# A recurrence kernel's small triangular solves on GpSimd alone, with permuted head slots and two masked evictions

## Chip, cores and metric

One core of a Trainium2 chip runs the whole program. The metric is the device time of one execution in microseconds, lower is better. Engines: TensorE (PE), VectorE (DVE), ScalarE (ACT), GpSimd (POOL), SyncE (SP, which here only issues DMAs).

## What is computed

A two-layer backbone on 2048 tokens of width 1024, with a prefix of 256 context tokens. The first layer is a bidirectional RWKV-7 recurrence with 16 heads of 64, the second a multi-head latent attention. The part that matters here is the recurrence, run over the context tokens and then over the others, forward and backward in time:

```python
def step(s, inp):                       # s: (direction, batch, head, 64, 64)
    r_t, lw_t, k_t, v_t, a_t, b_t = inp
    sa = jnp.einsum('dbhij,dbhj->dbhi', s, a_t)
    s = s * jnp.exp(lw_t)[..., None, :] + sa[..., None] * b_t[..., None, :] + v_t[..., None] * k_t[..., None, :]
    return s, jnp.einsum('dbhij,dbhj->dbhi', s, r_t)
```

In front of it stand the projections of r, k, v and the decays, behind it a normalisation, a gate and an output projection.

## The kernel before

The work goes through stages that overlap a little. **Projection** (project_block): a context block of 256 tokens, then four blocks of 512. In a block, PE multiplies in units of 128 channels, first the k units, then r and v. Each product is made of three matmuls with split operands: activations lh + ll, weights whi + wlo. ScalarE casts whi and lh, GpSimd or DVE subtracts to get wlo (L418) and ll (L493). The k units also give, per direction, the chunk matrices that the scan needs (GpSimd: kd L627, kb L630, the copy EC L620).

**Scan** (scan): the recurrence in chunks. One iteration advances each direction by 32 tokens: x (L1122, from the state S), u (L1132, multiplies x by a triangular inverse), the next state s (L1150), y (L1160). The state tile svu holds for each head the old state, the loaded v and the copied u, and s contracts over all of it. Ahead of each chunk aa (L1092) makes 16 products of 64x64, which are evicted times a mask into the tile big (L1097), and tr (L1106) makes transposes, which ScalarE evicts (L1110). EC is the decay by which s is evicted (L1153). PE's order is written by hand: per iteration the steps of one direction stand between those of the other, with matmuls of another task as filler. The filler is the gate's projection in iterations 0 to 47 (weights f_whi by ScalarE, f_wlo L695 on DVE and L696 on GpSimd, three buffers each), then the readout (L790 and after). The other engines are ordered by a scheduler from priorities; keep_in_program_order pins an instruction against it.

**Solve**: four chunks of 32 tokens in two directions and 16 heads make 128 systems of 32x32, one per partition. solve(n) loads their matrix Lt (L987), sets N to the identity and in 31 steps adds to N's later columns a product of one column of N with one row of Lt: a multiply (L1002) and an add (L1006) per step. Rows 0 to 5 of N (Na, tmpa) are on DVE, rows 6 to 31 (Nb, tmpb) on GpSimd, and the multiplies of even steps are pinned to the program's order. solve is a generator: its caller takes two steps at a time between other work, solves 0 and 1 during the projection (L546, L576), solve n+2 during the four iterations after the start of n. N goes to memory and comes back transposed as tt (load_tt). There are 18 solves, and the scan waits for none of them but through tt.

The u copies (L1138 on DVE, L1140 on ScalarE) write heads in steps of two slots:

```python
dst = S[ur, e, cls // 2:8:2, :]
```

so the DVE copy of a half and the ScalarE copy of the same half interleave in one region of the tile.

Of the kernel before, what the change touches and what calls it, by code (L numbers as in the profile page):

```python
# [43 lines left out]
PIN = 0  # L44
# [64 lines left out]
def revlast(ap):  # L109
    step, n = ap.ap[-1]  # L110
    return bass.AP(ap.tensor, ap.offset + step * (n - 1), [list(x) for x in ap.ap[:-1]] + [[-step, n]])

# [9 lines left out]
class Build:  # L122
# [348 lines left out]
    def project_block(self, t0, W, bp, wp, tp, pp, ind, indt, smask, w2d, sol):  # L471
# [85 lines left out]
        def v_unit(f, lh, ll):  # L557
# [15 lines left out]
            for e in range(2):  # L573
                nc.sync.dma_start(self.vtok[t0:t0 + W, e, f, :].rearrange("(n p) d -> p n d", p=P), vk[:, :W // P, e * 64:(e + 1) * 64])
# [8 lines left out]
        for f in range(KT):  # L583
# [13 lines left out]
            for d in range(2):  # L597
# [22 lines left out]
                nc.gpsimd.tensor_copy(self.EC[d][:, f, c0:c0 + nch], E[:, :nch, 32 - one])  # L620
# [362 lines left out]
    def solve(self, n):  # L983
        nc, sp, Nd = self.nc, self.svp, self.Nd
        JS = 6
        L = sp.tile([P, 32, 32], F32, name="Lt")
        nc.sync.dma_start(L.rearrange("p s t -> p (s t)"), self.Ld[n])  # L987
        Na = sp.tile([P, JS, 32], F32, name="Na")
        Nb = sp.tile([P, 32 - JS, 32], F32, name="Nb")
        nc.gpsimd.memset(Na, 0.0)  # L990
        nc.gpsimd.memset(bass.AP(Na.tensor, Na.offset, [Na.ap[0], [33, JS]]), 1.0)
        nc.gpsimd.memset(Nb, 0.0)
        nc.gpsimd.memset(bass.AP(Nb.tensor, Nb.offset + JS, [Nb.ap[0], [33, 32 - JS]]), 1.0)
        for s in range(31):
            for eng, N, j0, j1 in ((nc.vector, Na, 0, min(s + 1, JS)), (nc.gpsimd, Nb, JS, s + 1)):
                k = j1 - j0
                if k <= 0:
                    continue
                w = 31 - s
                tmp = sp.tile([P, 160 if j0 == 0 else 176], F32, name="tmpa" if j0 == 0 else "tmpb")  # L1000
                tv = tmp[:, :k * w].rearrange("p (j t) -> p j t", t=w)
                op = eng.tensor_tensor(tv, N[:, 0:k, s:s + 1].to_broadcast([P, k, w]),  # L1002
                                       L[:, s, s + 1:32].unsqueeze(1).to_broadcast([P, k, w]), ALU.mult)
                if s % 2 == PIN:
                    self.tc.keep_in_program_order(op)
                eng.tensor_tensor(N[:, 0:k, s + 1:32], N[:, 0:k, s + 1:32], tv, ALU.add)  # L1006
            if s % 2:
                yield
        yield
        nc.sync.dma_start(Nd[n % 2][0:JS].rearrange("j p t -> p j t"), Na)  # L1010
        nc.sync.dma_start(Nd[n % 2][JS:32].rearrange("j p t -> p j t"), Nb)
# [9 lines left out]
    def scan(self, upto):  # L1021
        nc, ins, tc = self.nc, self.ins, self.tc
        JS = 6
        HP_CHAIN, HP_AA = 3000, 1500
        with ExitStack() as top:
# [55 lines left out]
            def aa(d, i):  # L1081
# [5 lines left out]
                with tc.high_priority(HP_AA):  # L1087
                    ps = [pp.tile([P, 4, 64], F32, name="ps_aa", bufs=3) for _ in range(2)]
                    for p in range(8):
                        for e in range(2):  # L1090
                            o, r = slice(64 * ((e + p + 1) % 2), 64 * ((e + p + 1) % 2) + 64), slice(64 * e, 64 * e + 64)
                            nc.tensor.matmul(ps[e][o, p // 2, :], kb[r, p, ck], B[r, 2 * p + e, 0, ck], start=True, stop=True)  # L1092
                    for e in range(2):
                        r = slice(64, 128) if e == 0 else slice(0, 64)
                        for p0 in range(2):
                            o = slice(64 * ((e + p0 + 1) % 2), 64 * ((e + p0 + 1) % 2) + 64)
                            nc.vector.tensor_tensor(B[r, 2 * p0 + e::4, 0, ck], ps[e][o], amask[o, d:d + 1, :].to_broadcast([64, 4, 64]), ALU.mult)  # L1097
# [19 lines left out]
            def x_of(d, i):  # L1117
                (B, k), S = big(d, i), SVU[d][i % 2]
                xp = pp.tile([P, 4, 64], F32, name="ps_xu", bufs=2)
                for h in range(NH):  # L1120
                    r = slice(32 * (h % 4), 32 * (h % 4) + 32)
                    nc.tensor.matmul(xp[r, h // 4, :], B[:, h, 0, k:k + 32], S[:, h % 2, h // 2, :], start=True, stop=True)  # L1122
# [793 lines left out]
```

## Time and profile before

| what | value |
|---|---|
| runs | 5520.90, 5520.99, 5532.20 us; median 5520.99 |
| profiled execution | 5527.81 us, span 5526.0 us, mean granted clock 0.922 |
| PE / PE weight load | 4724.3 us (85%) / 3434.1 us (62%) |
| DVE / ACT / POOL | 3784.7 us (68%) / 2186.3 us (40%) / 2752.4 us (50%) |
| projection, scan, then latent attention | to about 1326, 1331 to about 2750, to 5526 us |

Busy times are those of the whole span, and the stages differ: what a change in one stage is worth is read from that stage. A row of the waits says how long an engine stood still and which instruction released it. Idle time of an engine for which nobody waits costs nothing.

### The profile page before, as it was taken

The page shows a single profiled execution, that of the slowest core. Times are in us where ns is not written, and L with a number is a line of the kernel's source. Part 1 is how long each engine was busy: PE and PEld are TensorE (multiplying, and loading weights), DVE is VectorE, ACT ScalarE, POOL GpSimd, SP SyncE. Part 2 cuts the span into 40 slices and gives each one's busy share as a digit, 9 for nine tenths or more (in the row PEclk, how much of TensorE's full clock was granted, in tenths as well). Part 3 has the DMA queues.
Part 4 walks back from the last instruction along what each step waited for, and adds up shares of the span by engine and source line. Part 5 has one row for each costly group of instructions (what it writes and reads, how often), then busy time and mean ns, then how long its engine had stood idle before and what let it go on. Part 6 is the DMA issues. An engine that isn't in the chain of part 4 may idle for free.

```text
span 5526.0 us, 123424 instructions
## 1 busy us (share of the span) xinstructions
PE 4724.3 (85%) x50559; PEld 3434.1 (62%) x50559; DVE 3784.7 (68%) x6213; ACT 2186.3 (40%) x3862; POOL 2752.4 (50%) x2473
## 2 busy tenths in 40 slices
PE   6778787887878887677789998699999999999999
PEld 4655555555767776466667876555555555555567
DVE  5989897875888888786565443266666666666644
ACT  4444444443544444333333343233333333333332
POOL 2575656463544444343254452255656655656551
PEclk8889898887989999788889999889999999999999
DMA  7655555556776666868788767621111111011023
GB/s 220 188 168 171 162 165 172 165 169 188 212 214 175 186 178 168 243 196 235 229 247 256 246 163 237 235 76 54 30 50 58 28 51 57 23 58 32 25 91 104
DMA packets 1006881, 818.59 MB, mean 148 GB/s; under 512 B 280885, under 2 KB 876420, under 8 KB 994794
## 3 DMA queue, kind: packets, MB, share of 16 engines
q1 hardware_dynamic: 872046, 734.48, 44.5%
q10 hardware_dynamic: 134188, 75.95, 5.0%
q8 instruction: 397, 6.50, 0.5%
q14 instruction: 170, 1.39, 0.1%
q0 software_dynamic: 80, 0.26, 0.0%
HBM read 551.84 MB, written 258.66 MB: 147 GB/s over the span
## 4 chain that ended last, share of the span: by engine, by line
PE 31%; DVE 9%; DMA 3%; ACT 2%; issue 2%; POOL 2%; SPq 1%; ACTq 0%; DVEq 0%; POOLq 0%
PE ps_o L1729 9%; PE ps_s L1706 7%; PE ps_p L1680 4%; DVE mx L1684 3%; DVE ri L1745 2%; DVE acc L1722 1%; PE ps_a L1387 1%; PE ps_a L1388 1%; PE ps_a L1389 1%; ACT pt L1708 1%; PE ps_o L1882 1%; PE ps_o L1884 1%; PE ps_o L1883 1%; DVE acc L1719 1%; PE ps_p L1694 1%
## 5 line engine op out<-in xcount | busy, mean ns | idle before, releaser
L1722 POOL TENSOR_TENSOR acc<-acc,pt 128x1024 f32<-128x1024 f32 x352 | 867.2, 2464 | 406.5 <-ACT pt L1708 386.5
L1684 DVE TENSOR_REDUCE mx<-ps_p 128x1 f32<-128x512 f32 x1024 | 661.5, 682 | 356.8 <-PE ps_p L1680 356.7
L1708 ACT ACTIVATE pt<-ps_s 128x1024 f32<-128x1024 f32 x576 | 591.0, 1026 | 779.8 <-PE ps_s L1706 737.6
L1706 PE MATMUL ps_s<-qr,a_kr 64*128 64x512 f32 (+1 forms) x2304 | 524.6, 393 | 5.8 <-ACT qr L1697 4.0
L1729 PE MATMUL ps_o<-pt,av 128*64 128x512 f32 x2304 | 523.3, 599 | 0.0
L1680 PE MATMUL ps_p<-knh,qnh 64*128 64x512 f32 (+1 forms) x1280 | 369.9, 404 | 99.3 <-DVE mx L1684 48.9
L500 PE MATMUL ps_r<-lh,whi 128*128 128x512 f32 (+1 forms) x960 | 386.4, 404 | 37.0 <-ACT lh L492 33.4
L418 POOL TENSOR_TENSOR wlo<-wraw,whi 128x1024 fp32r<-128x1024 f32 (+3 forms) x120 | 265.7, 2215 | 300.2 <-ACT whi L414 293.8
L501 PE MATMUL ps_r<-ll,whi 128*128 128x512 f32 (+1 forms) x960 | 382.7, 400 | 15.4 <-DVE ll L493 11.9
L502 PE MATMUL ps_r<-lh,wlo 128*128 128x512 f32 (+1 forms) x960 | 379.6, 397 | 12.9 <-POOL wlo L418 7.1
L696 POOL TENSOR_TENSOR f_wlo<-f_wraw,f_whi 128x384 fp32r<-128x384 f32 x118 | 158.8, 1347 | 384.4 <-ACT f_whi L694 320.0
L1729 PEld LDWEIGHTS ps_o<-pt,av 128*64 128x64 f32 x2304 | 154.3, 137 | 296.3 <-issue 292.2
L1680 PE MATMUL ps_p<-a_kr,qr 64*128 64x512 f32 (+1 forms) x1280 | 329.5, 391 | 1.5 <-DMA qr<-qr 1.5
L1706 PEld LDWEIGHTS ps_s<-qr,a_kr 64*128 64x128 f32 (+1 forms) x2304 | 289.9, 185 | 64.3 <-DVE qr L1697 15.2
L1680 PEld LDWEIGHTS ps_p<-knh,qnh 64*128 64x128 f32 x1280 | 184.3, 189 | 196.8 <-DVE mx L1684 132.2
L480 DVE SCALAR_TENSOR_TENSOR lerp<-xx,cols,hb 128x512 f32<-128x512 f32 (+1 forms) x240 | 239.3, 1022 | 88.2 <-POOL ll L493 67.9
L1706 PE MATMUL ps_s<-qnh,knl 64*128 64x512 f32 x1152 | 283.0, 417 | 4.3 <-ACT pt L1708 4.2
L1150 PE MATMUL ps_s<-svu,big 128*64 128x64 f32 x4544 | 236.7, 247 | 52.0 <-DVE svu L1138 30.3
L1706 PE MATMUL ps_s<-qnh,knh 64*128 64x512 f32 x1152 | 267.5, 389 | 0.0
L1706 PE MATMUL ps_s<-qnl,knh 64*128 64x512 f32 x1152 | 267.4, 389 | 0.0
L1097 DVE TENSOR_TENSOR big<-ps_aa,amask 64x256 f32<-64x256 f32 x576 | 243.2, 422 | 29.7 <-PE ps_aa L1092 16.3
L1110 ACT COPY big<-ps_aa 64x256 f32<-64x256 f32 x576 | 211.0, 366 | 132.2 <-PE ps_aa L1106 126.2
(342 smaller groups left out, 12550.1 us busy)
## 6 DMA issues: line engine op xcount, KB each, us to landing
f_w<-wod SPq DMA_DIRECT2D x72, 1024.0 KB
wraw<-rwkv_w_in SPq DMA_DIRECT2D x120, 512.0 KB
kbt<-KB SPq DMA_DIRECT2D x72, 512.0 KB
big<-AR SPq DMA_DIRECT2D x144, 256.0 KB
AR<-ar SPq DMA_DIRECT2D x64, 512.0 KB
KB<-kb SPq DMA_DIRECT2D x64, 512.0 KB
f_wraw<-rwkv_w_in SPq DMA_DIRECT2D x64, 512.0 KB
f_wraw<-mla_w_in SPq DMA_DIRECT2D x54, 512.0 KB
```

The costliest lines, as they stand in the source:

```text
L418: eng.tensor_tensor(lo[:, k0:k1, :], raw[:, k0:k1, :], hi[:, k0:k1, :].bitcast(F32), ALU.subtract)
L480: nc.vector.scalar_tensor_tensor(L[:, :W], xx[:, k, :W], col["mu"][:, j * 8 + k:j * 8 + k + 1], hb[:, k, 1:W + 1], ALU.mult, ALU.add)
L500: nc.tensor.matmul(ps, hi[:, k, :], lh[k][:, :W], start=k == 0, stop=False)
L501: nc.tensor.matmul(ps, hi[:, k, :], ll[k][:, :W], start=False, stop=False)
L502: nc.tensor.matmul(ps, lo[:, k, :], lh[k][:, :W], start=False, stop=k == KT - 1)
L1097: nc.vector.tensor_tensor(B[r, 2 * p0 + e::4, 0, ck], ps[e][o], amask[o, d:d + 1, :].to_broadcast([64, 4, 64]), ALU.mult)
L1680: nc.tensor.matmul(ps[h2][:, o * kw:(o + 1) * kw], x[r, t * P:(t + 1) * P], y[r, k0:k0 + kw], start=st, stop=not st)
L1684: nc.vector.tensor_reduce(mx[:, h2, t, n % 4:n % 4 + 1], ps[h2], mybir.AxisListType.X, ALU.max)
L1706: nc.tensor.matmul(ps[:, h2, :], x[r, ks], y[r, :], start=i == 0, stop=i == 4)
L1708: nc.scalar.activation(pt, ps, AF.Exp, scale=SCALE)
L1722: eng.tensor_tensor(a, a, pt, ALU.add)
L1729: nc.tensor.matmul(st["po"][hs, :], st["v"][:, kt, hs], pt[:, h2, :], start=kt == 0, stop=kt == NK - 1)
```

## The change

The solve no longer splits N's rows. One tile Nt (32x32 per partition) and one temporary tmpn of 256 elements, all 62 operations on GpSimd, two memsets instead of four, one store instead of two; no instruction is pinned. The heads of svu, EC and the token copy of v take a permuted slot, 4(f mod 2) + f div 2, so a u copy writes four slots in a row: DVE's and ScalarE's halves are separate. aa writes the eight products of one operand half into one PSUM tile of 64 partitions (two of the four 64x64 quarters of the array instead of four), and each of two evictions takes a 64x512 region instead of four that take 64x256.

```diff
--- before.py
+++ after.py
@@ -41,7 +41,6 @@
 BREAK = 1000
 GB = 288
 FW, FS, FF = 2, 1, 1
-PIN = 0
 MU = 2
 
 _SHAPES = {
@@ -109,6 +108,10 @@
 def revlast(ap):
     step, n = ap.ap[-1]
     return bass.AP(ap.tensor, ap.offset + step * (n - 1), [list(x) for x in ap.ap[:-1]] + [[-step, n]])
+
+
+def slot(f):
+    return 4 * (f % 2) + f // 2
 
 
 def chunked(ap):
@@ -571,7 +574,7 @@
             vk = tp.tile([P, 4, P], F32, name="vk", tag="ta", bufs=2)
             nc.vector.tensor_copy(vk.rearrange("p n m -> p (n m)")[:, :W], pt[:, :W])
             for e in range(2):
-                nc.sync.dma_start(self.vtok[t0:t0 + W, e, f, :].rearrange("(n p) d -> p n d", p=P), vk[:, :W // P, e * 64:(e + 1) * 64])
+                nc.sync.dma_start(self.vtok[t0:t0 + W, e, slot(f), :].rearrange("(n p) d -> p n d", p=P), vk[:, :W // P, e * 64:(e + 1) * 64])
             next(sh[0], None)
             next(sol, None)
 
@@ -617,7 +620,7 @@
                 nc.scalar.activation(E[:, :nch, inc:inc + 32], chunked(cs[:, :W]), AF.Exp, scale=-KAPPA / 2)
                 Ei = tp.tile([P, 512], F32, name="Ei", bufs=2)
                 nc.scalar.activation(Ei[:, :W], cs[:, :W], AF.Exp, scale=KAPPA / 2)
-                nc.gpsimd.tensor_copy(self.EC[d][:, f, c0:c0 + nch], E[:, :nch, 32 - one])
+                nc.gpsimd.tensor_copy(self.EC[d][:, slot(f), c0:c0 + nch], E[:, :nch, 32 - one])
                 ar = tp.tile([P, 16, 64], F32, name="ar", bufs=2)
                 nc.vector.scalar_tensor_tensor(rc(ar[:, :nch, 0:32]), chunked(kkh[:, :W]), -2.0, E[:, :nch, exc:exc + 32], ALU.mult, ALU.mult)
                 nc.vector.tensor_tensor(ar[:, :nch, 32:64], chunked(psr[:, :W]), E[:, :nch, inc:inc + 32], ALU.mult)
@@ -981,34 +984,23 @@
         self.TT = {}
 
     def solve(self, n):
-        nc, sp, Nd = self.nc, self.svp, self.Nd
-        JS = 6
+        nc, sp, eng = self.nc, self.svp, self.nc.gpsimd
         L = sp.tile([P, 32, 32], F32, name="Lt")
         nc.sync.dma_start(L.rearrange("p s t -> p (s t)"), self.Ld[n])
-        Na = sp.tile([P, JS, 32], F32, name="Na")
-        Nb = sp.tile([P, 32 - JS, 32], F32, name="Nb")
-        nc.gpsimd.memset(Na, 0.0)
-        nc.gpsimd.memset(bass.AP(Na.tensor, Na.offset, [Na.ap[0], [33, JS]]), 1.0)
-        nc.gpsimd.memset(Nb, 0.0)
-        nc.gpsimd.memset(bass.AP(Nb.tensor, Nb.offset + JS, [Nb.ap[0], [33, 32 - JS]]), 1.0)
+        N = sp.tile([P, 32, 32], F32, name="Nt")
+        eng.memset(N, 0.0)
+        eng.memset(bass.AP(N.tensor, N.offset, [N.ap[0], [33, 32]]), 1.0)
         for s in range(31):
-            for eng, N, j0, j1 in ((nc.vector, Na, 0, min(s + 1, JS)), (nc.gpsimd, Nb, JS, s + 1)):
-                k = j1 - j0
-                if k <= 0:
-                    continue
-                w = 31 - s
-                tmp = sp.tile([P, 160 if j0 == 0 else 176], F32, name="tmpa" if j0 == 0 else "tmpb")
-                tv = tmp[:, :k * w].rearrange("p (j t) -> p j t", t=w)
-                op = eng.tensor_tensor(tv, N[:, 0:k, s:s + 1].to_broadcast([P, k, w]),
-                                       L[:, s, s + 1:32].unsqueeze(1).to_broadcast([P, k, w]), ALU.mult)
-                if s % 2 == PIN:
-                    self.tc.keep_in_program_order(op)
-                eng.tensor_tensor(N[:, 0:k, s + 1:32], N[:, 0:k, s + 1:32], tv, ALU.add)
+            k, w = s + 1, 31 - s
+            tmp = sp.tile([P, 256], F32, name="tmpn")
+            tv = tmp[:, :k * w].rearrange("p (j t) -> p j t", t=w)
+            eng.tensor_tensor(tv, N[:, 0:k, s:s + 1].to_broadcast([P, k, w]),
+                              L[:, s, s + 1:32].unsqueeze(1).to_broadcast([P, k, w]), ALU.mult)
+            eng.tensor_tensor(N[:, 0:k, s + 1:32], N[:, 0:k, s + 1:32], tv, ALU.add)
             if s % 2:
                 yield
         yield
-        nc.sync.dma_start(Nd[n % 2][0:JS].rearrange("j p t -> p j t"), Na)
-        nc.sync.dma_start(Nd[n % 2][JS:32].rearrange("j p t -> p j t"), Nb)
+        nc.sync.dma_start(self.Nd[n % 2].rearrange("j p t -> p j t"), N)
 
     def load_tt(self, n):
         nc = self.nc
@@ -1020,7 +1012,6 @@
 
     def scan(self, upto):
         nc, ins, tc = self.nc, self.ins, self.tc
-        JS = 6
         HP_CHAIN, HP_AA = 3000, 1500
         with ExitStack() as top:
             top.enter_context(tc.manual_schedule(engines={mybir.EngineType.PE}))
@@ -1085,16 +1076,14 @@
                 ck = slice(k0, k0 + 64)
                 kb = KBh[(d, i // 2)]
                 with tc.high_priority(HP_AA):
-                    ps = [pp.tile([P, 4, 64], F32, name="ps_aa", bufs=3) for _ in range(2)]
+                    ps = [pp.tile([P, 8, 64], F32, name="ps_aa", bufs=3) for _ in range(2)]
                     for p in range(8):
                         for e in range(2):
-                            o, r = slice(64 * ((e + p + 1) % 2), 64 * ((e + p + 1) % 2) + 64), slice(64 * e, 64 * e + 64)
-                            nc.tensor.matmul(ps[e][o, p // 2, :], kb[r, p, ck], B[r, 2 * p + e, 0, ck], start=True, stop=True)
+                            o, r = slice(64 - 64 * e, 128 - 64 * e), slice(64 * e, 64 * e + 64)
+                            nc.tensor.matmul(ps[e][o, p, :], kb[r, p, ck], B[r, 2 * p + e, 0, ck], start=True, stop=True)
                     for e in range(2):
-                        r = slice(64, 128) if e == 0 else slice(0, 64)
-                        for p0 in range(2):
-                            o = slice(64 * ((e + p0 + 1) % 2), 64 * ((e + p0 + 1) % 2) + 64)
-                            nc.vector.tensor_tensor(B[r, 2 * p0 + e::4, 0, ck], ps[e][o], amask[o, d:d + 1, :].to_broadcast([64, 4, 64]), ALU.mult)
+                        o = slice(64 - 64 * e, 128 - 64 * e)
+                        nc.vector.tensor_tensor(B[o, e::2, 0, ck], ps[e][o], amask[o, d:d + 1, :].to_broadcast([64, 8, 64]), ALU.mult)
 
             def tr(d, m, half):
                 if m >= NCH // 2:
@@ -1119,7 +1108,7 @@
                 xp = pp.tile([P, 4, 64], F32, name="ps_xu", bufs=2)
                 for h in range(NH):
                     r = slice(32 * (h % 4), 32 * (h % 4) + 32)
-                    nc.tensor.matmul(xp[r, h // 4, :], B[:, h, 0, k:k + 32], S[:, h % 2, h // 2, :], start=True, stop=True)
+                    nc.tensor.matmul(xp[r, h // 4, :], B[:, h, 0, k:k + 32], S[:, h % 2, slot(h // 2), :], start=True, stop=True)
                 X[d] = sp.tile([P, 4, 64], F32, name="xs")
                 nc.scalar.copy(X[d], xp)
 
@@ -1133,7 +1122,7 @@
                 for cls in range(4):
                     e = cls % 2
                     ur = slice(96, 128) if e == 0 else slice(32, 64)
-                    dst = S[ur, e, cls // 2:8:2, :]
+                    dst = S[ur, e, cls // 2 * 4:cls // 2 * 4 + 4, :]
                     if cls < 2:
                         nc.vector.tensor_copy(dst, up[32 * cls:32 * cls + 32, :, :])
                     else:
@@ -1147,7 +1136,7 @@
                 ps = pp.tile([P, 8, 64], F32, name="ps_s", bufs=1)
                 for h in range(NH):
                     e = h % 2
-                    nc.tensor.matmul(ps[e * 64:(e + 1) * 64, h // 2, :], B[:, h, 1, k:k + 64], S[:, e, h // 2, :], start=True, stop=True)
+                    nc.tensor.matmul(ps[e * 64:(e + 1) * 64, slot(h // 2), :], B[:, h, 1, k:k + 64], S[:, e, slot(h // 2), :], start=True, stop=True)
                 for e in range(2):
                     r = slice(e * 64, (e + 1) * 64)
                     nc.vector.tensor_tensor(nx[r, e, :, :], ps[r, :, :], self.EC[d][r, :, c:c + 1].to_broadcast([64, 8, 64]), ALU.mult)
@@ -1157,7 +1146,7 @@
                 yp = pp.tile([P, 4, 64], F32, name="ps_xu", bufs=2)
                 for h in range(NH):
                     cls, q = h % 4, h // 4
-                    nc.tensor.matmul(yp[32 * cls:32 * cls + 32, q, :], B[:, h, 0, k + 32:k + 64], S[:, h % 2, h // 2, :], start=True, stop=True)
+                    nc.tensor.matmul(yp[32 * cls:32 * cls + 32, q, :], B[:, h, 0, k + 32:k + 64], S[:, h % 2, slot(h // 2), :], start=True, stop=True)
                 ys = sp.tile([P, 4, 64], F32, name="ys")
                 nc.scalar.copy(ys, yp)
                 ylate.append(lambda: nc.scalar.dma_start(self.yd[c // 4][c % 4, d].rearrange("k t x -> (k t) x"), ys.rearrange("p q d -> p (q d)")))
```

On GpSimd, in the first full block of the projection, where the k units end; wlo is a weight split, tmpb and Nb are the solve's two operations, ll the split of an activation. Before:

```order
L418 TENSOR_TENSOR wlo<-wraw,whi 128x1024
L1002 TENSOR_TENSOR tmpb<-Nb,Lt 128x133
L1006 TENSOR_TENSOR Nb<-Nb,tmpb 128x7x19
L1002 TENSOR_TENSOR tmpb<-Nb,Lt 128x144
L1006 TENSOR_TENSOR Nb<-Nb,tmpb 128x8x18
L418 TENSOR_TENSOR wlo<-wraw,whi 128x1024
L1002 TENSOR_TENSOR tmpb<-Nb,Lt 128x153
L1006 TENSOR_TENSOR Nb<-Nb,tmpb 128x9x17
L1002 TENSOR_TENSOR tmpb<-Nb,Lt 128x160
L1006 TENSOR_TENSOR Nb<-Nb,tmpb 128x10x16
L493 TENSOR_TENSOR ll<-lerp,lh 128x512
L418 TENSOR_TENSOR wlo<-wraw,whi 128x1024
```

and now, at the last rows ahead of the same ll (tmpn and Nt are the solve):

```order
L999 TENSOR_TENSOR Nt<-Nt,tmpn 128x28x4
L997 TENSOR_TENSOR tmpn<-Nt,Lt 128x87
L999 TENSOR_TENSOR Nt<-Nt,tmpn 128x29x3
L997 TENSOR_TENSOR tmpn<-Nt,Lt 128x60
L999 TENSOR_TENSOR Nt<-Nt,tmpn 128x30x2
L997 TENSOR_TENSOR tmpn<-Nt,Lt 128x31
L999 TENSOR_TENSOR Nt<-Nt,tmpn 128x31
L496 TENSOR_TENSOR ll<-lerp,lh 128x512
L421 TENSOR_TENSOR wlo<-wraw,whi 128x1024
```

These are the last operations of solve 1, which stood in the second block before. Between two wlo there are now up to 20 solve operations, and 124 of them ahead of this ll.

On GpSimd, at the end of the projection (the v units' wlo, then the scan's svu memsets). Before:

```order
L418 TENSOR_TENSOR wlo<-wraw,whi 128x640
L627 TENSOR_TENSOR kd_12082<-kd_12082,kT 128x512
L655 TENSOR_TENSOR kd_12051<-kd_12051,kd_12082 128x512
L620 COPY EC_144<-E 128x16
L630 TENSOR_TENSOR kb<-kd_12082,Ei 128x16x32
L418 TENSOR_TENSOR wlo<-wraw,whi 128x640 x6
L1047 MEMSET svu_12610 128x1024
L1047 MEMSET svu_12611 128x1024
```

and now:

```order
L999 TENSOR_TENSOR Nt<-Nt,tmpn 128x29x3
L997 TENSOR_TENSOR tmpn<-Nt,Lt 128x60
L999 TENSOR_TENSOR Nt<-Nt,tmpn 128x30x2
L997 TENSOR_TENSOR tmpn<-Nt,Lt 128x31
L999 TENSOR_TENSOR Nt<-Nt,tmpn 128x31
L421 TENSOR_TENSOR wlo<-wraw,whi 128x640 x2
L1038 MEMSET svu_12452 128x1024
L1038 MEMSET svu_12453 128x1024
```

The six wlo in a row now have solve 2 among them: 11 operations ahead of the second, 19 ahead of the third and of the fourth, 13 ahead of the last two.

On GpSimd, in the scan's first part (f_wlo and p_lo are splits for the fillers). Before, at the start of a solve:

```order
L696 TENSOR_TENSOR f_wlo<-f_wraw,f_whi 128x384
L1002 TENSOR_TENSOR tmpb<-Nb,Lt 128x25
L1006 TENSOR_TENSOR Nb<-Nb,tmpb 128x25
L1002 TENSOR_TENSOR tmpb<-Nb,Lt 128x48
L1006 TENSOR_TENSOR Nb<-Nb,tmpb 128x2x24
L1002 TENSOR_TENSOR tmpb<-Nb,Lt 128x69
L1006 TENSOR_TENSOR Nb<-Nb,tmpb 128x3x23
L1002 TENSOR_TENSOR tmpb<-Nb,Lt 128x88
L1006 TENSOR_TENSOR Nb<-Nb,tmpb 128x4x22
L1002 TENSOR_TENSOR tmpb<-Nb,Lt 128x105
L1006 TENSOR_TENSOR Nb<-Nb,tmpb 128x5x21
L1002 TENSOR_TENSOR tmpb<-Nb,Lt 128x120
```

and now, at the middle of a solve:

```order
L999 TENSOR_TENSOR Nt<-Nt,tmpn 128x15x17
L997 TENSOR_TENSOR tmpn<-Nt,Lt 128x256
L999 TENSOR_TENSOR Nt<-Nt,tmpn 128x16x16
L997 TENSOR_TENSOR tmpn<-Nt,Lt 128x255
L999 TENSOR_TENSOR Nt<-Nt,tmpn 128x17x15
L699 TENSOR_TENSOR f_wlo<-f_wraw,f_whi 128x384
L997 TENSOR_TENSOR tmpn<-Nt,Lt 128x252
L999 TENSOR_TENSOR Nt<-Nt,tmpn 128x18x14
L997 TENSOR_TENSOR tmpn<-Nt,Lt 128x247
L999 TENSOR_TENSOR Nt<-Nt,tmpn 128x19x13
L997 TENSOR_TENSOR tmpn<-Nt,Lt 128x240
```

Before, 12 to 16 solve operations stand between two such splits; now 31 stand in a row twice, with one f_wlo between.

## Rows read from the trace of the kernel before

**Rows 1.** Busy time by stretch: engines' time (instructions), granted clock, DMA share, GB/s.

```profile
230.00:1340.00 1110.00, 895.68 (x7335) 633.73 (x7339) 923.69 (x1038) 495.95 (x844) 649.00 (x539) 0.88 0.55 168
1340.00:2220.00 880.00, 721.01 (x17551) 620.02 (x17549) 727.35 (x1687) 408.60 (x993) 408.20 (x757) 0.90 0.71 190
2220.00:2750.00 530.00, 380.73 (x8643) 315.93 (x8631) 374.26 (x869) 188.29 (x492) 184.74 (x303) 0.85 0.78 227
2750.00:5526.00 2776.00, 2571.65 (x15750) 1742.26 (x15750) 1592.96 (x2311) 987.53 (x1309) 1421.09 (x762) 0.97 0.34 106
```

**Rows 2.** PE's waits, 1340 to 2220: releaser, total us, times, longest us.

```profile
PE ps_s L1150 <- DVE svu L1138: 30.0, 28, 2.7
PE ps_aa L1092 <- DVE big L1097: 27.2, 19, 2.2
```

**Rows 3.** Busy time in two single iterations of the scan.

```profile
1441.48:1453.78 12.30, 12.12 (x358) 10.57 (x352) 8.93 (x20) 7.33 (x18) 3.23 (x8) 1.00 0.76 184
1453.78:1473.73 19.95, 15.76 (x376) 13.79 (x376) 15.51 (x39) 7.95 (x19) 6.93 (x14) 1.00 0.81 240
```

**Rows 4.** The same view for tile tmpa alone, so DVE's solve; last row 48 iterations.

```profile
1441.48:1453.78 12.30, 0.66 (x3) 1.00 0.76 184
1453.78:1473.73 19.95, 6.68 (x21) 1.00 0.81 240
...
1658.30:1671.80 13.50, 1.05 (x5) 1.00 0.43 102
...
1376.50:2193.20 816.70, 240.49 (x725) 0.91 0.70 189
```

**Rows 5.** Groups of instructions, 1340 to 2220: busy us, mean ns, idle before.

```profile
L1097 DVE TENSOR_TENSOR big<-ps_aa,amask 64x256 f32<-64x256 f32 x392 | 165.5, 422 | 20.6 <-PE ps_aa L1092 12.3
...
L1153 DVE TENSOR_TENSOR svu<-ps_s,EC 64x512 f32<-64x512 f32 x194 | 133.2, 687 | 6.9 <-PE ps_s L1150 3.6
...
L696 POOL TENSOR_TENSOR f_wlo<-f_wraw,f_whi 128x384 fp32r<-128x384 f32 x64 | 79.6, 1244 | 278.2 <-ACT f_whi L694 218.2 <-PE ps_s L1150 25.3 <-PE ps_g L726 15.2
```

**Rows 6.** PE's timeline in one iteration: start us, us, instruction.

```profile
1448.85 0.69 PE L1092 MATMUL ps_aa<-big,kbt 64*64 64x64 f32 x32
1449.47 1.15 PE L1150 MATMUL ps_s<-svu,big 128*64 128x64 f32 x32
```

**Rows 7.** GpSimd's groups by shape, 1340 to 2220.

```profile
L1002 POOL TENSOR_TENSOR tmpb<-Nb,Lt 128x168 f32<-128x168 f32 x24 | 12.8, 533 | 1.9
...
L1002 POOL TENSOR_TENSOR tmpb<-Nb,Lt 128x25 f32<-128x25 f32 x24 | 6.9, 286 | 0.3
```

**Rows 8.** Busy time in projection blocks one to three, tile tmpb, GpSimd's solve.

```profile
230.10:507.90 277.80, 31.12 (x50) 0.89 0.56 173
507.90:789.20 281.30, 29.90 (x50) 0.88 0.55 166
789.20:1060.40 271.20, 0.00 (x0) 0.89 0.55 169
```

**Rows 9.** GpSimd's timeline at the end of block one's k units.

```profile
299.77 0.47 POOL L1002 TENSOR_TENSOR tmpb<-Nb,Lt 128x153 f32<-128x153 f32 x1
300.31 0.48 POOL L1006 TENSOR_TENSOR Nb<-Nb,tmpb 128x153 f32<-128x153 f32 x1
...
302.42 1.29 POOL L493 TENSOR_TENSOR ll<-lerp,lh 128x512 fp32r<-128x512 f32 x1 [0.46 <-PE ps_r L501]
```

**Rows 10.** GpSimd's timeline at the end of the projection.

```profile
1285.72 1.93 POOL L418 TENSOR_TENSOR wlo<-wraw,whi 128x640 fp32r<-128x640 f32 x1 [8.19 <-ACT whi L414]
...
1314.49 1.93 POOL L418 TENSOR_TENSOR wlo<-wraw,whi 128x640 fp32r<-128x640 f32 x1 [4.05 <-ACT whi L414]
```

**Rows 11.** SyncE's queue, two stretches: the loads of Lt.

```profile
238.75 0.33 SPq L987 DMA_DIRECT2D Lt<-Ld  x1
...
1286.32 0.32 SPq L987 DMA_DIRECT2D Lt<-Ld  x1
```

**Rows 12.** ScalarE's waits, 1340 to 2220.

```profile
ACT svu L1140 <- DVE svu L1138: 127.1, 69, 4.8
```

## Prediction

> **What bounds the kernel now.** I read the stages first, as busy time by stretch [rows 1]. The change touches three of them: the projection (230 to 1340 us), and the scan with the gate's weights as its filler (1340 to 2220) and then with the readout as its filler (2220 to 2750). The last row, half of the span, holds nothing that the change edits. In the scan's first part no engine is full: PE 721 us of 880, DVE 727, POOL 408. The reader is to see two nearly equal loads that wait for each other in turn. What PE waits for there [rows 2] is DVE: 30.0 us for the copies of u (L1138), 27.2 us for the masked products (L1097). What DVE does besides shows in single iterations. One that starts at 1441.48 lasts 12.30 us, and PE is busy for 12.12 of them; the next lasts 19.95, with PE busy for 15.76 and DVE for 15.51 [rows 3]. The two differ in the solve on DVE: 0.66 us against 6.68 [rows 4]. So DVE's 31 solve steps stand between PE and the links of the chain.
>
> **GpSimd's price for a solve.** Before, GpSimd does 50 operations of 5,850 elements per solve, afterwards 62 of 10,912 (two for each step s, of (s+1)(31−s) elements). Rows of the shapes 25 and 168 give 286 and 533 ns [rows 7]: 243 ns and 1.73 ns per element. An operation that starts at 299.77 lasts 0.47, and the next starts at 300.31 [rows 9], so 0.07 us lies between two. 62 × 0.313 + 10,912 × 0.00173 = 38.3 us. Every shape above 169 elements is taken along that line; no row shows one. I take 36 to 39.5 us; the upper end of doubt is 48, since the 50 operations of the first full block needed 31.1 us [rows 8], a third more than the same line gives (22.3).
>
> **Part A, the first full block of the projection.** The order on GpSimd no longer has four solve operations between two splits of weights (wlo): both solves 0 and 1 stand ahead of the last splits of the k units and of the ll that ends them. Lt is asked for at 238.75 [rows 11] and I take it to land 3 us later (an estimate; no row times it). From then GpSimd has 2 × 36 us of solve, eight wlo of about 2.4 us (19), four ll (6) and five small operations (5) ahead of that ll: 241.5 + 102 = 343.5, or 350.5 with 39.5 per solve. I take 347. Before, that ll ended at 302.42 + 1.29 = 303.7 [rows 9]. PE cannot hide it, since each k unit needs its wlo: **+43**. Given back: the second block carried solve 1 and took 281.30, the third without a solve 271.20 [rows 8], so −10; and −2 for the solve steps that leave the rest of the first block. Net **+31**, bounds +26 and +55 (at 48 per solve).
>
> **Part B, the end of the projection.** Solve 2 stood in the scan; now it is ahead of the last five wlo of the v units. Those were 1.93 us each, with the first of six at 1285.72 and the sixth at 1314.49, and GpSimd idle in between [rows 10]. Lt is queued at 1286.32 [rows 11], so solve operations can start at about 1290; all 62, and the wlo in between, end at 1290 + 38 + 6 = 1334, and the sixth wlo ends near 1338 against 1316.4. The last v unit starts about 3 us behind its wlo or as soon as PE is through: **+17**, bounds +12 and +24. It isn't given back at the scan's start, where this solve wasn't waited for.
>
> **Part C, the scan's first part.** Three things change in each of its 48 iterations (817 us, 17.0 each [rows 4]).
> - The solve leaves DVE: 240.5 us in 725 operations [rows 4], 5.0 per iteration. How much of it is on the path? The two iterations above give (19.95 − 12.30)/(6.68 − 0.66) = 1.3 us per us, but the second also waits for a load. A straight line through the lengths of 42 such windows, with the number of fill units as a second variable, gives 0.40 us per us. I take that: −2.0, bounds −1.0 and −3.0.
> - The masked products: four evictions of 422 ns become two of twice the size. The nearest row is the state's eviction of the same size at 687 ns [rows 5], so 1.69 becomes 1.37 us. The u copies no longer write interleaved slots of one tile half each, so ScalarE's pair need not wait for DVE's: it waited 127.1 us for them, 69 times [rows 12]. Together −0.7 per iteration, bounds −0.3 and −1.2, for only part of these waits reach PE (30.0 and 27.2 us [rows 2], 1.2 per iteration).
> - PE itself gets more to do. The 16 products of aa now use two 64×64 quarters of the array instead of four. Before, the 32 instructions last 0.69 us; the state's 32, which fill two column halves, last 1.15 [rows 6]. Two aa per iteration: **+0.92**, bounds 0 (the nearest row could be the same row) and +1.4.
>
> The sum is −2.0 − 0.7 + 0.9 = −1.8 per iteration; −1.65 with some of it lost to loads, which stay: 48 × −1.65 = **−80**, bounds −130 and −30. GpSimd has to carry 38 us of solve per four iterations beside five f_wlo of 1.24 [rows 5] and about 10 us of other work and store waits: some 55 of 62 to 66 us. It is late only if its order is bad (rival 1).
>
> **Part D, the scan's second part.** The readout's loads and its own chain set the pace here, and 530 us hold PE work of 381 [rows 1]. Twenty-four iterations bring +22 us of aa, half of it under waits (+11), DVE is relieved (−12), and lumps of 8 to 28 solve operations stand ahead of r_y's work (0 to +25): **+10**, bounds −15 and +30.
>
> Everything behind 2750 us is left as it is: DVE and GpSimd are free of the solve there in both.
>
> **Sum.** +31 + 17 − 80 + 10 = −22. The profiled execution took 5527.8; its own sum is 5506. The three runs have their median at 5521.0, 6.8 below it, and I put the change on that: **5499**, say 5498. The forecast's own range is 5466 to 5533, with the parts' doubts taken together. A difference below 0.2% (11 us) can't be told from none.
>
> **A rule against the change.** In the first full block, with DVE busy for 924 of the stage's 1110 us [rows 1], the 50 solve operations took 31.1 us [rows 8] where the line of the scan's rows gives 22.3. The Trainium skill, GPSIMD Engine Reference, §1 Specifications and §4.1 Engine selection, says that GpSimd shares its SBUF interfaces with VectorE and that an elementwise operation with two inputs belongs on VectorE, since GpSimd is about twice as slow. By that rule alone, as an estimate, moving DVE's 20 us per solve would cost GpSimd 40, which would make a solve 62 us and GpSimd the bound. The trace prices the added part at 12 us (38.3 less the 25.8 that the same line with its gaps gives for 50 operations), since it is few, long operations. Nothing in the sum uses the rule.
>
> **Rivals.**
> 1. *GpSimd's lumps hold up the fillers* (slower). In the scan 31 solve operations now stand without a break, half a solve, 18 to 20 us, with a single f_wlo between the halves. Sixty-four fill units passed in 880 us [rows 5], one per 13.8; at the forecast's pace it is one per 12.3. Three buffers let GpSimd run ahead by three. From the start of the first lump, 2 × 19.5 + 2 × 1.24 = 41.5 us pass until the second f_wlo behind it is there; PE asks for it after four units, 49 us, or some 45 if GpSimd was not fully ahead. The slack is 4 to 8 us, and it decides at 21 to 23 us per half solve. Then PE waits in each cycle of four iterations, and all that DVE's relief and the copies give is lost: part C comes to about −20 + 17 of such waits, near 0. Time: 5521 + 31 + 17 + 0 − 5 = 5564. For it: the narrow slack, and contention that a third more per operation in block 1 shows. Against it: the slack is there by the rows' prices. **0.20**.
> 2. *PE is the bound* (about the same). Only the waits that DVE ends vanish (57 us [rows 2], and as an estimate some 43 more in the links behind them), aa's 66 us (144 × 0.46) are paid in full, so the scan gives about −36: 5521 + 31 + 17 − 36 = 5533. The Trainium skill, TensorEngine Tiling (Array Packing), Tiling Modes and Key Properties, says that the 64×64 mode has four tiles and that different tiles run loads and matmuls in parallel, so two of them idle in the new form. For it: PE at 82% of the stage. **0.10**.
> 3. *More DVE time is on the path than 0.40* (faster). If iterations come to 14 us, near the 12.30 and 13.50 of those almost without a solve on DVE [rows 4] plus 0.9 of aa, the scan gives −125: 5521 + 48 − 125 = 5444. Against it: fills of 1.5 us each and loads (svu, kbt) stay. **0.20**.
>
> The forecast has **0.50**. Faster by over 0.2% takes two thirds of it (0.34) and rival 3: 0.54. Same: 0.13 of the forecast and 0.04 of rival 2: 0.17. Slower: rival 1, the rest of rival 2 and of the forecast: 0.29. The range, 5440 to 5570, reaches to rivals 1 and 3, for each holds a fifth; before the result I leave 0.1 outside at either end.
>
> **What would show it.** Right: the k phase of block 1 ends near 347 instead of 304, with PE idle before L502 for POOL's wlo; the scan begins some 48 us later than 1340; its first part takes about 800 us instead of 880, ACT's wait for DVE's copies is gone and aa's 32 instructions last about 1.15 us. Wrong: PE waits of many us for f_wlo in the scan (rival 1), a DVE at 60% with iterations still at 17 us (rival 2), or iterations at 14 (rival 3). If block 1 isn't longer, part A's reading of GpSimd's order fails.

## The result, and the profile after it

The changed kernel takes 5606.6 us (median of 4 runs, 5595.0 to 5612.2) against 5520.9 before: a ratio of 1.0149, interval 1.0126 to 1.0172, slower by 86 us between the medians. The forecast was 5498, the range ended at 5570, and the side was wrong. Rival 1, with 5564, is the mechanism that came, at a higher price. The profiled execution has a span of 5608.5 us. Its stages, in the view of busy time by stretch (columns as in [rows 1]); the stretches are cut at the same PE instructions as those of before, the n-th of one against the n-th of the other, since PE's order hardly differs:

```profile
230.00:559.10 329.10, 238.74 (x1873) 168.12 (x1872) 221.94 (x240) 125.66 (x215) 221.33 (x241) 0.83 0.49 150
559.10:830.30 271.20, 223.60 (x1810) 158.62 (x1809) 225.10 (x233) 124.95 (x210) 146.03 (x106) 0.89 0.55 168
1438.50:2263.60 825.10, 697.74 (x16908) 618.79 (x16904) 441.42 (x715) 389.94 (x948) 495.83 (x811) 0.92 0.72 187
2263.60:2819.00 555.40, 389.04 (x8600) 326.62 (x8597) 276.32 (x517) 184.32 (x485) 224.03 (x335) 0.83 0.75 212
```

The scan's two parts before:

```profile
1376.50:2193.20 816.70, 686.59 (x16913) 594.17 (x16905) 700.46 (x1626) 389.30 (x946) 395.98 (x745) 0.91 0.70 189
2193.20:2722.40 529.20, 374.48 (x8599) 307.94 (x8595) 373.42 (x882) 185.15 (x485) 179.64 (x301) 0.84 0.78 224
```

The first full block went from 277.8 to 329.1 us, the second from 281.3 to 271.2 [rows 8]. In the first one PE was busy for 238.7 us where the same instructions took 223.5, at a granted clock of 0.83 against 0.89; for the other 36 us it stood idle. The scan's first part takes 825.1 us against 816.7, although DVE is busy for 441 us there instead of 700. This stretch holds 47 iterations (x of the first one starts at 1341.5 us, ahead of it), not 48 as [rows 4] has it: 17.4 us each before. The second part takes 555.4 against 529.2.

GpSimd's timeline shows the first loss. Two pieces of it, at the start and at the end of the k units of block one:

```profile
243.03 0.68 POOL L997 TENSOR_TENSOR tmpn<-Nt,Lt 128x60 f32<-128x60 f32 x1
...
357.25 0.29 POOL L997 TENSOR_TENSOR tmpn<-Nt,Lt 128x60 f32<-128x60 f32 x1
...
358.55 1.28 POOL L496 TENSOR_TENSOR ll<-lerp,lh 128x512 fp32r<-128x512 f32 x1
```

The ll that stood at 302.42 [rows 9] stands at 358.55, behind both solves. PE's waits in that block (230 to 560 us) now begin with the weight splits, which had 0.2 us of them before:

```profile
PE ps_r L505 <- POOL wlo L421: 37.2, 8, 8.0
```

And in the scan (1403 to 2264 us) PE's waits for DVE [rows 2] are nearly gone, but their place is taken:

```profile
PE ps_g L729 <- POOL f_wlo L699: 63.4, 14, 9.0
```

One such wait, first on GpSimd (the solve's last operation ahead of the split, the split) and then on PE (the matmul that waited 9.00 us):

```profile
1612.45 0.65 POOL L997 TENSOR_TENSOR tmpn<-Nt,Lt 128x247 f32<-128x247 f32 x1
1613.05 0.99 POOL L699 TENSOR_TENSOR f_wlo<-f_wraw,f_whi 128x384 fp32r<-128x384 f32 x1
```

```profile
1614.10 0.61 PE L729 MATMUL ps_g<-f_h,f_wlo 128*128 128x288 f32 x1 [9.00 <-POOL f_wlo L699]
```

From 1588.5 to 1613.1 GpSimd did 37 solve operations with no f_wlo among them, and PE stood still for the last third of that time.

### The profile page after: what moved, and what is told of

Its sections match the earlier page's. It is cut to its first block, busy times and chain, and to the rows that moved or that the text cites. A ratio compares the mean times of both kernels' runs of the same rounds, so it can differ in the third digit from the quotient of the medians.

```text
span 5608.5 us, 122290 instructions
## 1 busy us (share of the span) xinstructions
PE 4763.8 (85%) x50559; PEld 3485.7 (62%) x50559; DVE 3379.6 (60%) x4809; ACT 2186.5 (39%) x3862; POOL 2942.7 (52%) x2653
## 4 chain that ended last, share of the span: by engine, by line
PE 30%; DVE 9%; DMA 3%; ACT 3%; issue 2%; POOL 2%; SPq 1%; ACTq 0%; POOLq 0%; DVEq 0%
PE ps_o L1718 9%; PE ps_s L1695 7%; PE ps_p L1669 4%; DVE mx L1673 3%; DVE ri L1734 2%; DVE acc L1711 1%; ACT pt L1697 1%; PE ps_o L1871 1%; PE ps_o L1873 1%; PE ps_o L1872 1%; PE ps_a L1376 1%; PE ps_a L1377 1%; PE ps_a L1378 1%; DVE acc L1708 1%; DMA r_y<-yd 1%
## 5 line engine op out<-in xcount | busy, mean ns | idle before, releaser
L503 PE MATMUL ps_r<-lh,whi 128*128 128x512 f32 (+1 forms) x960 | 390.9, 409 | 38.7 <-ACT lh L495 31.1
L997 POOL TENSOR_TENSOR tmpn<-Nt,Lt 128x31 f32<-128x31 f32 (+15 forms) x558 | 295.4, 529 | 101.5 <-DMA Lt<-Ld 60.7
L999 POOL TENSOR_TENSOR Nt<-Nt,tmpn 128x31 f32<-128x31 f32 (+15 forms) x558 | 316.0, 566 | 41.6
L505 PEld LDWEIGHTS ps_r<-lh,wlo 128*128 128x128 f32 x960 | 201.8, 210 | 110.5 <-POOL wlo L421 64.2
```

Source lines behind the costliest of these rows:

```text
L503: nc.tensor.matmul(ps, hi[:, k, :], lh[k][:, :W], start=k == 0, stop=False)
L505: nc.tensor.matmul(ps, lo[:, k, :], lh[k][:, :W], start=False, stop=k == KT - 1)
```

## The experiments

Three things had changed at once: where GpSimd's operations stand, how many there are, and the forms of aa and of the u copies. The first four runs take them apart.

**The pins back.** The changed kernel, with one thing undone:

```diff
-            eng.tensor_tensor(tv, N[:, 0:k, s:s + 1].to_broadcast([P, k, w]),
+            op = eng.tensor_tensor(tv, N[:, 0:k, s:s + 1].to_broadcast([P, k, w]),
...
+            if s % 2 == 0:
+                self.tc.keep_in_program_order(op)
```

> The changed kernel with the even steps' multiplies of the solve pinned to the program's order again, all 62 operations still on GpSimd. Theory A (the loss is GpSimd's order: solves hoisted and lumped once nothing pins them): the first full block ends its k units near 315 us instead of 359 and the block lasts some 285 instead of 329; PE's wait for f_wlo in the scan falls from 63 us to under 15; the scan's first part takes 770 to 800 us; the whole 5430 to 5480. Theory B (the loss is the load, a solve of 38 us and more is too much for GpSimd wherever it stands): 5570 or more, waits for f_wlo stay above 40 us. Theory C (the two quarters of aa on PE cost the gain): between, 5510 to 5540, with the f_wlo wait gone.

5451.5 us, ratio to before 0.9875 (0.9853 to 0.9897): 155 us below the changed kernel, with all 62 operations of each solve still on GpSimd. GpSimd's order again has four solve operations between two weight splits in the projection and at most 16 between two f_wlo in the scan's first part. The same stretches (first block, scan's first part, second part):

```profile
229.70:509.80 280.10, 224.56 (x1873) 158.50 (x1872) 234.40 (x241) 125.40 (x215) 192.27 (x176) 0.89 0.57 172
1375.20:2156.80 781.60, 680.15 (x16912) 606.37 (x16908) 442.83 (x715) 390.36 (x947) 526.10 (x841) 0.94 0.74 197
2156.80:2656.60 499.80, 385.56 (x8600) 320.67 (x8600) 278.04 (x517) 185.19 (x487) 234.14 (x355) 0.87 0.84 237
```

GpSimd is busier in the scan's first part than in the changed kernel (526 against 496 us) and the part is 43.5 us shorter; PE's waits there do not name POOL's f_wlo at all. Theory A holds, B falls.

**The pins away, and nothing else.** The kernel before without its pins:

```diff
-                if s % 2 == PIN:
-                    self.tc.keep_in_program_order(op)
```

> The kernel before with the pins of the solve taken away and nothing else; the solve is still split between VectorE and GpSimd, slots and aa are as before. Theory A: the order alone costs, so it is slower than before by 30 to 80 us, with the first full block 30 us or more longer, though no operation was added. Theory B: within 15 us of before, since GpSimd's load is the same as before. Theory C: within 15 us of before.

5592.3 us, ratio 1.0121 (1.0099 to 1.0144): 72 us slower with not one operation more. The first block and PE's waits in it:

```profile
230.90:550.60 319.70, 235.74 (x1872) 164.52 (x1871) 263.92 (x364) 125.61 (x215) 193.12 (x221) 0.83 0.51 154
```

```profile
PE ps_r L502 <- POOL wlo L418: 28.0, 4, 13.3
```

The order costs by itself: the first block is 42 us longer than before, and the scan's second part takes 550 us against 529. The scan's first part is not longer:

```profile
1418.80:2234.00 815.20, 680.50 (x16912) 590.32 (x16910) 690.91 (x1578) 389.06 (x946) 363.74 (x701) 0.92 0.72 189
```

GpSimd has lumps of 36 to 50 solve operations there, 18.8 to 25.2 us, but behind each at most 14 more, 2 to 7 us, and PE's waits for its f_wlo come to 18.0 us in four. So in that part lumps of some 20 us are not enough for a loss (DVE's part of the solve is without pins here too); in the changed kernel a second one stands right behind the first.

**Slots and two evictions without the solve's move.** The kernel before, with the new slots and the new aa; the edit is that part of the change.

> The kernel before with its split, pinned solve, but with the permuted slots and the two evictions of aa. Theory A: 5490 to 5525, since the copies and evictions save 0.7 us per iteration and aa costs PE 0.9, part of it under waits; the projection stays within 5 us of before. Theory C (aa on two quarters is what ate the scan's gain): slower than before by 20 to 60 us. Theory B: as theory A.

5478.7 us, ratio 0.9926 (0.9901 to 0.9950): faster by 42, more than theory A gave it.

**aa back to four quarters**, in the changed kernel:

```diff
-                    ps = [pp.tile([P, 8, 64], F32, name="ps_aa", bufs=3) for _ in range(2)]
+                    ps = [pp.tile([P, 4, 64], F32, name="ps_aa", bufs=3) for _ in range(2)]
...
-                            nc.tensor.matmul(ps[e][o, p, :], kb[r, p, ck], B[r, 2 * p + e, 0, ck], start=True, stop=True)
+                            nc.tensor.matmul(ps[e][o, p // 2, :], kb[r, p, ck], B[r, 2 * p + e, 0, ck], start=True, stop=True)
```

> The changed kernel with aa on four quarters and its four evictions of 64x256 again. Theory A: the projection's 60 us stay lost and the scan gains at most 0.5 us per iteration, so 5565 to 5610. Theory C: the scan gains 40 to 66 us over the changed kernel, 5540 to 5565. Theory B: within 20 us of the changed kernel, 5590 to 5620.

5609.7 us, ratio to before 1.0160 (1.0140 to 1.0180): no difference from the changed kernel. PE's dearer aa is not what ate the gain; theory C falls. Its numbers lie in theory B's range too, but B has fallen with the first run.

The next four ask which lumps cost what, and where the 42 us came from.

**Pins for solves 0 and 1 alone** (`if n < 2 and s % 2 == 0`).

> The changed kernel with the pins back for solves 0 and 1 alone, those of the projection. Theory A1 (the projection's lumps and the scan's lumps cost separately): only the first full block comes back, 42 to 50 us: 5555 to 5570, the scan begins some 17 us later than before (solve 2 stays among the last splits of weights) and PE's wait for f_wlo stays near 60 us. Theory A2 (the scan is behind because the projection left it behind): the scan comes back too, 5470 to 5500.

5570.9 us (5553 to 5588), ratio 1.0094 (1.0064 to 1.0125). The first block is back (the second begins 0.4 us earlier than in the kernel before), the scan begins 14 us late with solve 2 still among the last splits, and its two parts last 819 and 552 us. PE's waits for f_wlo stay, 61.2 us.

**Pins for the solves from 2 on** (`if n >= 2 and s % 2 == 0`).

> The changed kernel with the pins back for the solves from 2 on alone. Theory A1: the first full block stays at some 329 us, solve 2 leaves the projection's end, the scan comes back: 5480 to 5500, that is the pinned kernel's 5451 plus the 42 us that the first block keeps. Theory A2: 5580 or more.

5492.2 us, ratio 0.9949 (0.9933 to 0.9966). The first block keeps its loss (the second begins 55 us late), the scan's parts last 778 and 498 us. The places cost separately, theory A1: 119 and 41 us above the pinned kernel one at a time, 155 together.

**The pinned kernel with aa on four quarters.**

> The pinned kernel (solve on GpSimd, even steps pinned, slots permuted) with aa on four quarters of the array and four evictions. Theory C2 (where PE is the bound in the scan, aa's 0.46 us per call is paid): faster than the pinned kernel by 20 to 60 us, 5390 to 5430. Theory D (DVE's two extra evictions per aa and PE's saving cancel, or other waits set the pace): within 12 us of 5451.

5455.3 us, ratio 0.9886 (0.9869 to 0.9904): theory D, no difference from 5451.5. With the solve off DVE the form of aa no longer shows in the whole time, either way.

**The slots alone**, in the kernel before:

```diff
-                    dst = S[ur, e, cls // 2:8:2, :]
+                    dst = S[ur, e, cls // 2 * 4:cls // 2 * 4 + 4, :]
```

(with the same permutation wherever heads of svu, EC and the token copy of v are addressed)

> The kernel before with the permuted slots alone. Theory E (the u copies' halves are what made the 42 us of slots and two evictions): 5480 to 5495, ScalarE's wait for DVE's copies in the scan's first part falls from 127 us to under 25. Theory F (the evictions made it): 5510 to 5520.

5523.4 us, ratio 1.0008 (0.9999 to 1.0017): nothing, and theory E falls. ScalarE's waits in the scan's first part (1340 to 2220 us) are as before; compare [rows 12]:

```profile
ACT svu L1143 <- DVE svu L1141: 124.5, 67, 4.7
```

ScalarE still waits for DVE's pair of copies, though the two write separate halves. Left in common are the PSUM tile ps_xu, which both read, and the tile svu, which both write in separate parts. In the pinned kernel, which has the new slots too, the copies follow each other just so, DVE's pair first, then ScalarE's:

```profile
1695.21 0.87 DVE L1129 COPY svu<-ps_xu 32x256 f32<-32x256 f32 x2
```

```profile
1696.11 0.75 ACT L1131 COPY svu<-ps_xu 32x256 f32<-32x256 f32 x2 [1.00 <-DVE svu L1129]
```

Which of the two tiles keeps the copies in order was not tried; that the slots don't part them is shown.

The last three settle the parts.

**Two evictions alone**, in the kernel before:

> The kernel before with the new form of aa alone (two quarters of the array, two evictions of 64x512); split pinned solve, slots as before. Theory F (the evictions made the 42 us of slots and two evictions, the slots nothing): 5473 to 5490, with the wait of PE for DVE at aa and s down by 20 us or more. Theory E2 (only both together): 5510 to 5525.

5482.0 us, ratio 0.9929 (0.9913 to 0.9946): theory F, 41 of the 42 us. In the scan's first part PE's waits for DVE at aa (27.2 us in [rows 2]) went to 2.6, and those at s from 30.0 to 22.6:

```profile
PE ps_s L1148 <- DVE svu L1136: 22.6, 25, 2.7
```

**The solve on GpSimd, pinned, alone**: the kernel before with the new solve and the pins, old slots, old aa.

> The kernel before with the solve wholly on GpSimd and its even steps pinned; slots and aa as before. Theory G (what counts is DVE's queue in the scan: the solve's leaving frees it, and then the form of aa no longer matters): 5448 to 5465, as the pinned kernel with aa on four quarters (5455). Theory H (gains add up): the pinned kernel without its 42 us, 5485 to 5505.

5465.1 us (5452.7 to 5467.7), ratio 0.9893 (0.9876 to 0.9911). Theory G by its numbers, at the edge; theory H falls, for the gains do not add up: 58 us from the solve alone and 41 from the evictions alone, 69 together. What the rest of the change adds to the solve's move, some 11 us, lies within overlapping intervals. The scan's parts last 781 and 502 us. ScalarE's wait for DVE's copies of u, with the old slots, is down to a sixth of [rows 12] (1340 to 2220 us):

```profile
ACT svu L1131 <- DVE svu L1129: 22.3, 36, 2.8
```

Most of that wait came from the solve in DVE's queue, not from the slots.

**All four u copies on ScalarE**, in the pinned kernel:

```diff
-                    if cls < 2:
-                        nc.vector.tensor_copy(dst, up[32 * cls:32 * cls + 32, :, :])
-                    else:
-                        nc.scalar.copy(dst, up[32 * cls:32 * cls + 32, :, :])
+                    nc.scalar.copy(dst, up[32 * cls:32 * cls + 32, :, :])
```

> The pinned kernel with all four copies of u on ScalarE. The copies of the two engines still follow each other (ScalarE's starts where DVE's pair ends), so four on one engine take 4 x 0.365 = 1.46 us where the two pairs take 0.86 + 0.74 = 1.60. Theory I (the link u to s is on the path, and DVE's queue delays its pair): faster than the pinned kernel by 10 to 30 us, 5420 to 5442. Theory J (loads and ScalarE's own queue set the pace): within 10 us of 5451, or slower.

5455.4 us, ratio 0.9881 (0.9863 to 0.9898): theory J. With DVE free, PE's waits in the scan are led by loads:

```profile
PE ps_xu L1113 <- DMA svu<-vtok: 37.2, 11, 9.4
```

So the best version is the change with the even steps pinned, 5451.5 us: 69 us faster than the kernel before and 155 faster than the kernel as changed. Its two variants at 5455 us, with aa on four quarters and with u on ScalarE, can't be told from it.

| kernel | solve on | pinned | aa, evictions | us | ratio |
|---|---|---|---|---|---|
| before | DVE + POOL | yes | 4 | 5520.9 | 1 |
| slots alone | DVE + POOL | yes | 4 | 5523.4 | 1.0008 |
| evictions alone | DVE + POOL | yes | 2 | 5482.0 | 0.9929 |
| pins away alone | DVE + POOL | no | 4 | 5592.3 | 1.0121 |
| solve alone, pinned | POOL | yes | 4 | 5465.1 | 0.9893 |
| change | POOL | no | 2 | 5606.6 | 1.0149 |
| change, pinned | POOL | yes | 2 | 5451.5 | 0.9875 |

## Why the prediction was wrong, point by point

- **Price of a solve: right in the scan, low in block one.** The by-shape rows of the scan after it stay within some 7% of the line past 169 elements; for the multiply of 256:

```profile
L997 POOL TENSOR_TENSOR tmpn<-Nt,Lt 128x256 f32<-128x256 f32 x11 | 7.2, 655 | 0.8
```

  243 + 256 × 1.73 = 686 ns was forecast for this shape; the add of the same size takes 733. In the scan the view for tile tmpn has 370.55 us for 682 operations, 543 ns each, so 33.7 us and some 4 us of gaps for 62: 38. In block one it has 75.74 us for 124, 611 ns each, so 42 with the gaps. The sign of that was in hand: 31.1 us against 22.3 [rows 8] is 40% more, not the third that the prediction names.
- **Part A: right in kind, a quarter low.** The first block became 51.3 us longer and the second gave back 10.1, net +41 where +31 stood, within its bounds. The ll that was put at 347 ended at 359.8; the dearer operations make some 9 of these 13 us, and the cause of the others stays open.
- **Part B: right.** Last split 1378.1 us against 1316.4; between the last r unit's end and the scan's start the kernel loses 18 us more than before (+17 forecast).
- **Part C: wrong, +8 in place of −80.** Two steps failed, and the pinned kernel parts them: with the pins the scan's first part gives −35 (816.7 to 781.6 us), and without them the lumps take 43.5 back.

  First, the slack. The prediction let GpSimd run three f_wlo ahead ("Three buffers let GpSimd run ahead by three") and so found 4 to 8 us in hand. Counted in the trace (f_wlo ended less units begun on PE), at the start of each solve's first lump from 1505 us on (eleven, of 31 to 41 operations and 18.8 to 26.8 us) GpSimd was one unit ahead seven times, two three times and none once. Its own input came late: behind the lump above it waits 7.63 us for ScalarE's f_whi, and of its 197.1 us of idle time ahead of f_wlo (1403 to 2264 us) f_whi ended 165.5. Units begin 13.3 us apart on average. From one unit ahead, PE asks for the first split behind a lump after one to two units, 13 to 27 us, and for the second after two to three, 27 to 40; by the prediction's own sum the second is there after 41.5. PE's 14 waits lie accordingly: five behind first lumps (22.4 us in all) and nine behind second ones (41.1). The kernel before without pins has the first lumps and hardly the second: 18.0 us, and no loss in this part. Buffers are a bound on running ahead, not a measurement of it; the row that told of it is in [rows 5], where f_whi ended 218.2 of 278.2 us.

  Second, 0.40 us per us of solve on DVE was too much; the line through 42 windows stands in no view. With everything else as before and the pins kept, taking 240 us of solve off DVE shortened the 47 iterations by 35 us (816.7 to 781.4), 0.15 per us, and PE's longest waits are then for loads (34.5 us for svu). The two iterations compared in [rows 3] differ in a load as well, which the text said and then did not price.
- **The u copies: wrong.** They are not parallel, and the −0.7 rested partly on that. The sign that was to show it, ScalarE's wait for DVE's copies gone, did come (13.6 us, 1403 to 2264), but by the solve's leaving. The two evictions alone carried the gain, some 41 us; in the profiled execution 16 and 15 us of it fall in the scan's two parts (801.1 and 514.4 us) and 9 behind it. They save DVE 0.31 us per aa (29.6 us of 700.5 in the first part); that all of this was on the path is not shown.
- **aa on PE: priced right, hardly paid.** The 32 matmuls do last 1.15 us in place of 0.69, as the two halves of [rows 6] said. The Trainium skill, TensorEngine Tiling (Array Packing), Key Properties, says that different tiles can run matmuls in parallel. The two durations agree with it. With four quarters the whole time is the same, in the changed and in the pinned kernel. In the profiled executions the scan's first part is some 12 us shorter with four quarters in both (813.4 against 825.1 and 768.8 against 781.6), 0.25 us per iteration where 0.92 stood, and most of that is lost again behind the scan; why was not found.
- **Part D: +26 where +10 stood**, inside its bounds. The missing pins again: pinned, the same part lasts 500 us, 29 less than before.
- **Nothing behind 2750: nearly.** Behind the scan (from 2722 us before) the changed kernel takes 14 us less than before. The seven kernels with two evictions take 5 to 14 us less, the other five with four between 6 less and 2 more. The cause stays open.
- **Slips that decide nothing.** Rival 3's iterations of 14 us give 48 × 3.0 = 144, not 125, and rival 1's sum has −5 where part D has +10, without a reason.

The sum that the runs give: +62 up to the first of the 47 iterations, of which the pins would have given back all, +8 and +26 in the scan, −14 behind it.

## What to carry to other kernels

When work moves to another engine, look at where the scheduler puts it, not only at how much it is: here the same operations cost 155 us more unpinned than pinned, and a plain removal of pins cost 72. A producer that feeds a loop of 13 us must not get 20 us of other work in one piece, and the same again behind its next delivery, unless the trace shows, by counting, that it is really ahead by that much. And change one thing at a time: of this change's three parts one is worth some 41 us by itself, one 58 and one nothing, 69 together, and the missing pins hid all of it.

## What the runs showed of the hardware

GpSimd's operations are not of one price. The 128x60 multiply takes 0.68 us at 243.03 and 0.29 at 357.25 in the same block. The same holds for the 62 operations of solve 0 and of solve 1 there (GpSimd's busy time for tile tmpn):

```profile
241.80:307.40 65.60, 43.37 (x62) 0.72 0.25 80
314.90:358.60 43.70, 32.37 (x62) 0.77 0.13 39
```

DVE was busy for 37.1 us of the first stretch. In the second it did nothing, since it waited for the ll behind the solve:

```profile
359.87 2.81 DVE L483 SCALAR_TENSOR_TENSOR lerp<-xx,cols,hb 128x512 f32<-128x512 f32 x1 [59.37 <-POOL ll L496]
```

The Trainium skill, GPSIMD Engine Reference, §1 Specifications, says that GpSimd shares its SBUF interfaces with VectorE. The two stretches agree with it, though ScalarE too was busier in the first (19.6 us against 8.2), and no run here varied DVE alone.

The granted clock in the scan's first part was 0.95 with the two evictions alone against 0.91 before, with PE busy for 701 of 801 us instead of 687 of 817. Between the pinned kernels with two evictions and with four it was 0.94 in both. How much of the gain of the evictions alone is the clock's and how much is DVE's was not separated.
